# Moving 26 gate projections of a hybrid decoder layer out of its attention heads, into a stage of their own

## The chip, the cores and the metric

The kernel runs on one core of one Trainium2 chip. A core has five engines with an instruction stream each: TensorE (PE in the profile, its weight loads as PEld), VectorE (DVE), ScalarE (ACT), GpSimd (POOL) and SyncE (SP), which here issues nearly all DMAs. Each stream is carried out in order; engines meet at semaphores. The metric is the device time of one execution in microseconds (us), lower is better; the time of a kernel is the median of its runs.

## The reference

One layer of a decoder trunk, fp32, batch 1, 1024 tokens of 1024 channels with 16 meta tokens ahead of them (1040 in all). Cut to what matters:

```python
h = rms_norm(x_with_meta, norm_mix)
proj = h @ w_in + b_in
(g_q, g_k, g_v, g_r, g_lr, m_q, m_k, m_v, m_o, m_i, m_f, gate_a, gate_b) = jnp.split(proj, splits, axis=-1)
o_gla = head_rms(gla(g_q, g_k, g_v, log_a(g_lr))) * silu(g_r)          # 4 heads, keys 128, values 256
o_ml  = head_rms(mlstm(conv(m_q), conv(m_k), m_v, m_i, m_f)) * sigmoid(m_o)   # 4 heads
y = sigmoid(gate_a) * (o_gla @ w_branch_gla) + sigmoid(gate_b) * (o_ml @ w_branch_ml)
x = x + y @ w_out
x = x + conv_ffn(rms_norm(x, norm_ffn))     # 1024 -> 2 x 2816 -> 1024, causal conv of width 3
out = rms_norm(x, norm_final)[:, 16:]
```

`g_r`, `m_o`, `gate_a` and `gate_b` are the gates: 1024 channels each, so 32 tiles of 128 channels. None of them enters the recurrences; they multiply what comes out of them.

## The kernel before

**Numbers.** fp32 values are split into a high part H (rounded by a copy on ACT) and a low part L (the difference, on DVE); a product is three matmuls, H x H, H x L and L x H. A weight unit (8 x 128 rows, 128 columns, 512 KB) is loaded into `wr` (2 buffers, issued by SP), split into `wH` and `wL` (3 buffers each) by `prep` (lines 102 to 107), and used by `proj_cm` (line 158, PSUM tag `pj`, 3 banks): three thirds of the tokens, each 8 x 3 = 24 matmuls. `proj_v` (lines 188 to 205, `pv`, the same banks) computes values with the tokens as rows.

**Stages.** After norm and transposes (to about 36 us) come the heads (to about 890), GLA heads 0 to 3 and then mLSTM heads 4 to 7. For a head, `head_proj` projects k, q and v, `gate_proj` the two tiles of its output gate (`r`, `g_r` or `m_o`), `merge_gate("a", s)` a tile of gate a; behind the last head eight tiles of gate b. Small projections for decay and mLSTM's gates (`lr`, evicted into `raw_s` at line 445) follow head 0's keys and queries. Then the branch products `bg` (gate a times o_gla W) and `bm` (L986), w_out (`po`), the FFN's up stage (22 pairs of channel tiles, each as two pieces of seven block products V, X, Y, Z, a Winograd form of the 2x2 block product, L1186) and its down stage (from 1690).

**The recurrences** run beside the projections. `gla(s)` and `mlstm(s)` are generators in the list `side`; `main(gen)` lets one step of `side` follow each step of a projection. A GLA head computes the decay logits (`pre`, L643), ACT and DVE make the log decays `la` and their cumulative sum `bc` (L646 to L652), and then, for levels 1, 2, 4 ... 64, factors `pk` (L679, L680, L684 on DVE, L681 on ACT, L683 on POOL), scores `sc` (L620 on PE), and a masked merge into `A` (L637 on DVE). `sct` (L613) transposes A when the levels below 64 are merged; `kh`, `k`, `qh` (L706 to L722) are decayed keys and queries. `post` (its transposes have the tag `s`) multiplies the result by its norm and, on DVE, by the gate `r`, and stores it to `osc`; gate a and b go to `gsc`. `load_o` brings `osc` back for `bg` and `bm`.

**Order.** A list scheduler takes the program as written, with priorities (`hp(PRI_...)` moves an instruction ahead by so many places), and writes out each engine's order before the run; at run time nothing is reordered.

**down_sums** forms block differences of `ffn_w_down` for the last stage, on the side: 11 loads of 1 MB into `ts` (L927), four subtractions each (L929), and two stores (L931) to `tdn`, eight during the gate b tiles, three during `bg`.

## Time and profile before

| | |
|---|---|
| median of 3 runs | 1927.97 us (1926.66 to 1928.35) |
| span of the profiled execution | 1924.5 us |
| time of the profiled execution, by the median | about 3.5 us more than its span |
| instructions | 31317 |
| busy: PE, DVE, ACT, POOL | 1895.0, 1114.7, 807.0, 213.2 us |
| DMA | 244.69 MB, mean 127 GB/s |

How to read it: a profile is one execution. "Busy" is the time in which an engine had an instruction running. The chain that ended last is followed back from the last instruction to what released each step; its shares by engine say what the time was made of. A row of a timeline has the start, the time, engine, line, operation, output<-inputs, shapes and a count, and in square brackets the idle time before it and what ended it.

### The profile page before, as it was taken

The page shows a single profiled execution, that of the slowest core. Times are in us where ns is not written, and L with a number is a line of the kernel's source. Part 1 is how long each engine was busy: PE and PEld are TensorE (multiplying, and loading weights), DVE is VectorE, ACT ScalarE, POOL GpSimd, SP SyncE. Part 2 cuts the span into 40 slices and gives each one's busy share as a digit, 9 for nine tenths or more (in the row PEclk, how much of TensorE's full clock was granted, in tenths as well). Part 3 has the DMA queues.
Part 4 walks back from the last instruction along what each step waited for, and adds up shares of the span by engine and source line. Part 5 has one row for each costly group of instructions (what it writes and reads, how often), then busy time and mean ns, then how long its engine had stood idle before and what let it go on. Part 6 is the DMA issues. An engine that isn't in the chain of part 4 may idle for free.

```text
span 1924.5 us, 31317 instructions
## 1 busy us (share of the span) xinstructions
PE 1895.0 (98%) x13065; PEld 1815.8 (94%) x13065; DVE 1114.7 (58%) x1662; ACT 807.0 (42%) x1254; POOL 213.2 (11%) x189
## 2 busy tenths in 40 slices
PE   8999999999999999999999999999999999999998
PEld 8999999999999999999999999999999999987776
DVE  6272634437535433642251445688878788786777
ACT  5153444344534423323520234544444344455573
POOL 3030301103000000000000000012222222200000
PEclk8999999999999999999999999999999999999999
DMA  5121112021132122574971433323333333388794
GB/s 166 35 57 37 55 38 76 23 80 34 55 103 69 55 78 55 191 230 138 293 272 48 132 121 127 125 77 111 113 120 110 110 110 114 96 296 322 280 371 161
DMA packets 210568, 244.69 MB, mean 127 GB/s; under 512 B 11710, under 2 KB 170960, under 8 KB 210427
## 3 DMA queue, kind: packets, MB, share of 16 engines
q1 hardware_dynamic: 208587, 240.85, 38.9%
q8 instruction: 102, 1.67, 0.4%
q10 hardware_dynamic: 1840, 1.85, 0.3%
q14 instruction: 39, 0.32, 0.1%
HBM read 185.72 MB, written 56.95 MB: 126 GB/s over the span
## 4 chain that ended last, share of the span: by engine, by line
PE 78%; DVE 7%; issue 5%; DMA 5%; ACT 2%; POOL 2%; SPq 0%; POOLq 0%; DVEq 0%; ACTq 0%
PE pj L158 20%; PE pv L201 7%; PE Y L1186 6%; PE X L1186 6%; PE Z L1186 6%; PE bm L986 5%; PE bg L986 5%; PE po L1287 4%; PE V L1186 3%; PE pdX L1436 3%; PE pdY L1436 2%; PE pdZ L1436 2%; DMA ts<-in_ffn_w_down_dram 1%; PE pdV L1436 1%; DMA tdn<-ts 1%
## 5 line engine op out<-in xcount | busy, mean ns | idle before, releaser
L158 PE MATMUL pj<-xH,wH_r 128*128 128x342 f32 (+2 forms) x392 | 126.5, 323 | 0.0
L158 PE MATMUL pj<-xH,wL_r 128*128 128x342 f32 (+2 forms) x392 | 124.3, 317 | 0.0
L158 PE MATMUL pj<-xL,wH_r 128*128 128x342 f32 (+2 forms) x392 | 124.0, 316 | 0.0
L205 DVE TENSOR_TENSOR v<-pv,bB 128x256 f32<-128x256 f32 x64 | 27.1, 423 | 117.5 <-PE pv L201 117.5
L683 POOL TENSOR_TENSOR pk<-pk,kT 128x256 f32<-128x256 f32 (+1 forms) x40 | 58.9, 1500 | 183.0 <-ACT pk L681 104.8
L201 PE MATMUL pv<-wH_gv,xH 128*128 128x256 f32 x256 | 76.0, 297 | 0.0
L201 PE MATMUL pv<-wH_mv,xH 128*128 128x256 f32 x256 | 75.1, 293 | 0.0
L158 PEld LDWEIGHTS pj<-xH,wH_r 128*128 128x128 f32 x392 | 73.8, 188 | 0.1
L158 PEld LDWEIGHTS pj<-xL,wH_r 128*128 128x128 f32 x392 | 73.8, 188 | 0.1
L158 PEld LDWEIGHTS pj<-xH,wL_r 128*128 128x128 f32 x392 | 73.7, 188 | 0.0
L1287 PE MATMUL po<-wH_wo,yH 128*128 128x256 f32 x256 | 72.2, 282 | 0.1
L201 PE MATMUL pv<-wL_mv,xH 128*128 128x256 f32 x256 | 72.0, 281 | 0.0
L201 PE MATMUL pv<-wL_gv,xH 128*128 128x256 f32 x256 | 72.0, 281 | 0.0
L201 PE MATMUL pv<-wH_mv,xL 128*128 128x256 f32 x256 | 71.9, 281 | 0.0
L1287 PE MATMUL po<-wL_wo,yH 128*128 128x256 f32 x256 | 71.6, 280 | 0.3 <-DVE wL_wo L107 0.3
L201 PE MATMUL pv<-wH_gv,xL 128*128 128x256 f32 x256 | 71.9, 281 | 0.0
L1287 PE MATMUL po<-wH_wo,yL 128*128 128x256 f32 x256 | 71.8, 281 | 0.0
L1235 DVE SCALAR_TENSOR_TENSOR cv<-u,fc,cv 128x1024 f32<-128x1024 f32 x44 | 65.3, 1484 | 0.4
L158 PE MATMUL pj<-xH,wH_ga 128*128 128x342 f32 x192 | 62.5, 326 | 0.0
L158 PE MATMUL pj<-xH,wH_gb 128*128 128x342 f32 x192 | 61.9, 322 | 0.0
L986 PE MATMUL bm<-omH,wL_bm 128*128 128x342 f32 x192 | 61.5, 320 | 0.0
L158 PE MATMUL pj<-xH,wL_gb 128*128 128x342 f32 x192 | 61.4, 320 | 0.0
(674 smaller groups left out, 6755.1 us busy)
## 6 DMA issues: line engine op xcount, KB each, us to landing
ts<-in_ffn_w_down_dram SPq DMA_DIRECT2D x11, 1024.0 KB, 6.2
tdn<-ts SPq DMA_DIRECT2D x22, 512.0 KB, 2.7
rg<-in_ffn_w_up_dram SPq DMA_DIRECT2D x22, 512.0 KB, 3.8
ru<-in_ffn_w_up_dram SPq DMA_DIRECT2D x22, 512.0 KB, 3.9
adr<-s SPq DMA_DIRECT2D x40, 256.0 KB, 3.0
rd<-in_ffn_w_down_dram SPq DMA_DIRECT2D x20, 512.0 KB, 8.5
do<-tdn SPq DMA_DIRECT2D x18, 512.0 KB, 5.8
wr_r<-in_w_in_dram SPq DMA_DIRECT2D x16, 512.0 KB, 4.0
```

Source lines behind the costliest of these rows:

```text
L158: nc.tensor.matmul(pt[:, :n], a[:, k, :], b[:, k, base + t0:base + t0 + n], start=(i == 0), stop=(i == 3 * NK - 1))
L201: nc.tensor.matmul(pt[:, :DV], a[:, k, t0:t0 + P], b[:, k % 4, :], start=(i == 0), stop=(i == 3 * NK - 1))
L205: nc.vector.tensor_tensor(vt[:n, c, :DV], pt[:n, :DV], bB[:n, :], OP.add)
L683: nc.gpsimd.tensor_tensor(e, e, k, OP.mult)
L986: nc.tensor.matmul(pt[:, i, :n], a[:, k, :], b[k][:, t0:t0 + n], start=(k == 0 and j == 0), stop=(k == NK - 1 and j == 2))
L1186: nc.tensor.matmul(out[:, :n], a[:, k, :], b, start=start and k == 0 and j == 0, stop=stop and k == 3 and j == 2, skip_group_check=True)
L1235: nc.vector.scalar_tensor_tensor(y, u[:, j:SEQ + j], fc[:, j, jj:jj + 1], y, OP.mult, OP.add)
L1287: nc.tensor.matmul(pt[:, :DV], a, b[:, k % 4, :], start=(k == 0 and i == 0), stop=(k == NK - 1 and i == len(terms) - 1))
L1436: nc.tensor.matmul(banks[r, j, b], p, q, start=first and k == 0, stop=last and k == 2, skip_group_check=True)
```

## The change

Of the 32 gate tiles, 26 (all of `g_r`, `m_o` and gate a, and gate b's tiles 4 and 5) leave the heads. They become 13 pairs in a new stage between the heads and `bg`, in the block form of the FFN's up stage: `piece` and `product` are now shared by both, and a pair is 2 x 7 products of 12 matmuls with 258 or 256 columns. Gate b's other six tiles stay in the old form: `TAIL` (0, 1, 2) behind the last head, `COVER` (3) at the entry of the new stage, `END` (6, 7) at its exit.

- The block form needs differences of token blocks: `token_sums(k)` makes them on POOL (two adds of 1026 columns, four subtractions of 514) and stores them to `tsc` (4 DMAs per k, on SP); `token_blocks` loads and splits them at the stage's entry. It needs sums of weights too: `gate_weights`.
- Heads store their outputs without gates to `osc`; `post` evicts on ACT with a scale instead of on DVE with a multiply by `r`. `gate_finish` loads `osc` back, applies Silu or Sigmoid with the bias, multiplies, and stores to `otd`, which `load_o` reads. Gate a and b get their bias with the later Sigmoid.
- Head 1's keys are projected beside head 0's keys and queries, where the first gate tile was.
- `PACE = 1.7`: 1.7 steps of `side` for one step of a projection, where it was one.
- `down_sums` becomes `half_sums`: two per pair in the first 11 pairs of the new stage, 512 KB each, through one buffer `ts`.

```diff
-    uk, uq, uv, ur, uga, ugb = {}, {}, {}, {}, {}, {}
...
+    TAIL, COVER, END = (0, 1, 2), (3,), (6, 7)
     def head_units(s):
-        h = s % 4
-        kq_units(s)
+        h, g, k, q = s % 4, "gm"[s // 4], (O_GK, O_MK)[s // 4], (O_GQ, O_MQ)[s // 4]
+        if s != 1:
+            uk[s] = u_cm(w_in, k + P * h, f"{g}k{h}")
+        uq[s] = u_cm(w_in, q + P * h, f"{g}q{h}")
         if s == 0:
-            ur[0] = [u_cm(w_in, O_GR, "r0_0")]
+            uk[1] = u_cm(w_in, O_GK + P, "gk1")
             uk["lr"] = U.add()
-        uv[s] = u_v((O_GV if s < 4 else O_MV) + DV * h, f"{'gm'[s // 4]}v{h}_")
-    def gate_units(s):
-        h = s % 4
-        o = (O_GR if s < 4 else O_MO) + DV * h
-        ur.setdefault(s, []).extend(u_cm(w_in, o + P * j, f"r{s}_{j}") for j in range(len(ur.get(s, ())), 2))
-    head_units(0)
+        uv[s] = u_v((O_GV if s < 4 else O_MV) + DV * h, f"{g}v{h}_")
     for s in range(8):
-        if GATE_LATER[s]:
-            kq_units(s + 1)
-        gate_units(s)
-        if s < 7:
-            head_units(s + 1)
-        uga[s] = u_cm(w_in, O_GA + P * s, f"ga{s}")
-    for j in range(NK):
+        head_units(s)
+    for j in TAIL + COVER:
         ugb[j] = u_cm(w_in, O_GB + P * j, f"gb{j}")
...
+    def key_proj(s):
+        hh = heads.setdefault(s, {})
+        kT = hh["k"] = hd.tile([P, T + 3], F32, name=f"kT{s}", tag="k", bufs=2)
+        return proj_cm(uk[s], TH_ALL if s > 1 else SEG_ALL, 0, lambda p, t0, n: nc.scalar.activation(
+            kT[:, t0:t0 + n], p, AF.Identity, bias=cc(C_GK + s)))
...
             if s == 0:
-                yield from together(pk, pq, gate_proj(0, (0,)))
+                yield from together(pk, pq, key_proj(1))
...
+    tsc = dram.tile([4, 4, P, 514], F32, name="tsc")
+    def token_sums(k):
+        a, b = (hd.tile([P, T], F32, name=f"x{i}{k}", tag="r", bufs=2) for i in "ab")
+        t = wp.tile([P, T], F32, name=f"tx{k}", tag="gst", bufs=1)
+        for y, i in ((a, k), (b, k + 4)):
+            nc.gpsimd.tensor_tensor(y[:, :NP], xH[:, i, T0:].bitcast(F32), xL[:, i, T0:].bitcast(F32), OP.add)
+        first, second = slice(0, 514), slice(512, NP)
+        t1, t2 = t[:, 0:514], t[:, 520:1034]
+        for dst, x, y in ((t1, a[:, second], a[:, first]), (t2, b[:, second], t1),
+                          (a[:, second], b[:, second], a[:, second]), (b[:, first], b[:, first], t2)):
+            nc.gpsimd.tensor_tensor(dst, x, y, OP.subtract)
+        for i, src in enumerate((t1, t2, a[:, second], b[:, first])):
+            nc.sync.dma_start(tsc[i, k], src)
...
-                nc.vector.scalar_tensor_tensor(of[:, a:b], tp.rearrange("p n w -> p (n w)"), ncols[j],
-                                               r[:, a:b], OP.mult, OP.mult)
+                nc.scalar.activation(of[:, a:b], tp.rearrange("p n w -> p (n w)"), AF.Copy, scale=ncols[j])
...
+    PACE = 1.7
+    due = [0.0]
+    def main(gen, pace=PACE):
         for _ in gen:
-            advance()
+            due[0] += pace
+            while due[0] >= 1:
+                due[0] -= 1
+                advance()
...
-    def down_sums(m, t):
-        nc.sync.dma_start(t.rearrange("p (k i) n -> p k (i n)", k=2), wsrc(w_dn, 2 * m, 2, 0, D))
-        for o, a, b in ((0, 1, 0), (1, 3, 1), (3, 3, 0), (2, 2, 3)):
-            nc.vector.tensor_tensor(t[:, o], t[:, a], t[:, b], OP.subtract)
-        for i in range(2):
-            nc.sync.dma_start(tdn[i][m], t[:, 2 * i:2 * i + 2])
     main(head_proj(0))
     for s in range(8):
         side.append((gla if s < 4 else mlstm)(s))
         if s == 3:
             side.append(small_rows())
-        nxt = head_proj(s + 1) if s < 7 else iter(())
-        if GATE_LATER[s]:
-            main(islice(nxt, 6))
-        main(gate_proj(s, (0, 1) if s else (1,)))
-        main(nxt)
-        main(merge_gate("a", s))
-    ts = hd.tile([P, NC + 1, DV + 1], F32, name="ts", tag="v", bufs=2).rearrange("p a b -> p (a b)")
-    for j in range(NK):
-        down_sums(j, ts[:, :2048].rearrange("p (i n) -> p i n", n=512))
-        main(merge_gate("b", j))
+        if s > 3:
+            token_sums(s - 4)
+        if s < 7:
+            main(head_proj(s + 1))
+    for j in TAIL:
+        main(merge_gate_b(j))
...
+    def product(out, a, b, n, start, stop):
+        for k in range(4):
+            for j, (x, y) in enumerate(((a[0], b[0]), (a[0], b[1]), (a[1], b[0]))):
+                nc.tensor.matmul(out[:, :n], x[:, k, :], y[:, k, :], start=start and k == 0 and j == 0,
+                                 stop=stop and k == 3 and j == 2, skip_group_check=True)
+    def piece(pool, name, p, us_, u2, A, B):
+        n = (W0, W1)[p]
+        V, X, Y, Z = (pool.tile([P, 512], F32, name=f"{b}{name}_{p}", tag=f"{b}{p}") for b in "VXYZ")
+        ug, uu = us_
+        u2 = u2[:, p, :n]
+        g1, g2 = (u[:, W0 * p:W0 * p + n] for u in (ug, uu))
+        e1, e2 = (u[:, 514 + 256 * p:770 + 256 * p] for u in (ug, uu))
+        h2 = slice(n - 256, n)
+        def prod(out, a, b, start, stop):
+            product(out, A[a], B(b, p), n, start, stop)
+        prod(V, "A12", "B21", True, True)
+        prod(X, "A11", "B11", True, True)
+        with hp(PRI_E):
+            nc.scalar.activation(g1, V[:, :n], AF.Copy)
+            nc.vector.tensor_tensor(g1, X[:, :n], g1, OP.add)
+        yield
+        prod(Y, "S1", "T1", True, True)
+        prod(Z, "S3", "T3", True, True)
+        yield
+        prod(X, "S2", "T2", False, True)
+        with hp(PRI_E):
+            nc.scalar.activation(u2, X[:, :n], AF.Copy)
+            nc.vector.tensor_tensor(e2, Y[:, h2], u2[:, h2], OP.add)
+            nc.vector.tensor_tensor(e2, Z[:, h2], e2, OP.add)
+        yield
+        prod(Y, "S4", "B22", False, True)
+        prod(Z, "A22", "T4", False, True)
+        with hp(PRI_E):
+            nc.vector.tensor_tensor(e1, Y[:, h2], u2[:, h2], OP.add)
+            nc.vector.tensor_tensor(g2, Z[:, :n], u2, OP.add)
+        yield
...
+    GATES = [(O_GR + P * j, C_GR + j, AF.Silu, "g", j) for j in range(NK)] + \
+            [(O_MO + P * j, C_MO + j, AF.Sigmoid, "m", j) for j in range(NK)] + \
+            [(O_GA + P * j, None, None, "a", j) for j in range(NK)] + \
+            [(O_GB + P * j, None, None, "b", j) for j in range(NK) if j not in TAIL + COVER + END]
+    NG = len(GATES) // 2
...
+    def gate_weights(q):
+        rg, ru = (wp.tile([P, NK, P], F32, name=f"gw{i}{q}", tag="wr", bufs=2) for i in range(2))
+        for r, g in ((rg, GATES[2 * q]), (ru, GATES[2 * q + 1])):
+            nc.sync.dma_start(r, wsrc(w_in, 0, NK, g[0], P))
+        sa, sb = (gs.tile([P, NK, P], F32, name=f"gs{x}{q}", tag=f"S{x}") for x in "AB")
+        def split(src, h, l):
+            nc.scalar.activation(h, src, AF.Copy)
+            nc.vector.tensor_tensor(l, src, h.bitcast(F32), OP.subtract)
+        def two(src, name):
+            h, l = (wp.tile([P, NK, P], F32R, name=f"g{p}{name}_{q}", tag="w" + p) for p in "HL")
+            split(src, h, l)
+            return [(h[:, 4 * i:4 * i + 4], l[:, 4 * i:4 * i + 4]) for i in range(2)]
+        a = WP[q] = {}
+        a["A11"], a["A12"] = two(rg, "A1")
+        yield
+        nc.vector.tensor_tensor(sa[:, 0:4], ru[:, 0:4], ru[:, 4:8], OP.add)
+        nc.vector.tensor_tensor(sa[:, 4:8], rg[:, 0:4], ru[:, 0:4], OP.subtract)
+        a["S1"], a["S3"] = two(sa, "SA")
+        yield
+        nc.vector.tensor_tensor(sb[:, 0:4], sa[:, 0:4], rg[:, 0:4], OP.subtract)
+        nc.vector.tensor_tensor(sb[:, 4:8], rg[:, 4:8], sb[:, 0:4], OP.subtract)
+        a["S2"], a["S4"] = two(sb, "SB")
+        yield
+        t = gs.tile([P, NK, P], F32R, name=f"gA22_{q}", tag="A22")
+        a["A22"] = t[:, 0:4], t[:, 4:8]
+        split(ru[:, 4:8], *a["A22"])
+        yield
...
+    def token_blocks():
+        for i in (0, 2, 1, 3):
+            h, l = TB[i] = [gs.tile([P, 4, 514], F32R, name=f"T{p}{i}", tag=f"T{p}{i}") for p in "HL"]
+            nc.sync.dma_start(l.bitcast(F32), tsc[i].rearrange("k p c -> p k c"))
+            nc.scalar.activation(h, l.bitcast(F32), AF.Copy)
+            nc.vector.tensor_tensor(l, l.bitcast(F32), h.bitcast(F32), OP.subtract)
...
+    def gate_finish(q):
+        for i, u in enumerate(gu.pop(q)):
+            _, c, f, g, j = GATES[2 * q + i]
+            if f is None:
+                nc.sync.dma_start(gsc[g][j], u[:, :NP])
+                continue
+            o = gs.tile([P, T], F32, name=f"go{q}_{i}", tag="o")
+            nc.sync.dma_start(o[:, :NP], osc[g][j])
+            nc.scalar.activation(u[:, :NP], u[:, :NP], f, bias=cc(c))
+            nc.vector.tensor_tensor(u[:, :NP], u[:, :NP], o[:, :NP], OP.mult)
+            nc.sync.dma_start(otd[g][j], u[:, :NP])
+    def half_sums(m, c):
+        t = gs.tile([P, 4, 256], F32, name=f"ts{m}{c}", tag="ts")
+        for k in range(2):
+            nc.sync.dma_start(t[:, 2 * k:2 * k + 2], w_dn[P * (2 * m + k):P * (2 * m + k + 1), :].rearrange(
+                "p (i n) -> p i n", i=2)[:, :, 256 * c:256 * c + 256])
+        for o, a, b in ((0, 1, 0), (1, 3, 1), (3, 3, 0), (2, 2, 3)):
+            nc.vector.tensor_tensor(t[:, o], t[:, a], t[:, b], OP.subtract)
+        for i in range(2):
+            nc.sync.dma_start(tdn[i][m][:, :, 256 * c:256 * c + 256], t[:, 2 * i:2 * i + 2])
+    def gate_bank(name):
+        return lambda t0: psG.tile([P, 512], F32, name=f"{name}_{t0}", tag=f"{'XYZ'[t0 // 342]}1")
+    token_blocks()
+    with hp(PRI_W):
+        for _ in range(3):
+            weights_step(0)
+    for j in COVER:
+        main(merge_gate_b(j, gate_bank(f"pc{j}")))
+    weights_step(0)
+    u2 = wp.tile([P, T], F32, name="gu2", tag="gst", bufs=1)[:, :2 * W0].rearrange("p (a b) -> p a b", b=W0)
+    behind_ = None
+    for q in range(NG):
+        gu[q] = [gs.tile([P, T], F32, name=f"gu{i}{q}", tag=f"u{i}", bufs=2) for i in range(2)]
+        for p in range(2):
+            g = piece(psG, f"g{q}", p, gu[q], u2, WP[q], gate_block)
+            next(g)
+            if p == 1:
+                weights_step(q + 1)
+            next(g)
+            if p == 1:
+                weights_step(q + 1)
+            if behind_:
+                next(behind_)
+            if p == 0 and q:
+                weights_step(q)
+                weights_step(q)
+                gate_finish(q - 1)
+            next(g)
+            behind_ = g
+        if q < NP2:
+            for i in range(2):
+                half_sums(q, i)
+    next(behind_)
+    for j in END:
+        ugb[j] = u_cm(w_in, O_GB + P * j, f"gb{j}")
+    gate_finish(NG - 1)
+    for j in END:
+        main(merge_gate_b(j, gate_bank(f"pe{j}")))
+    gs_ctx.close()
...
-            nc.sync.dma_start(l.bitcast(F32), osc[g][k])
+            nc.sync.dma_start(l.bitcast(F32), otd[g][k])
```

144 lines of the change are left out of this document (47 added, 97 removed).

## The prediction

> **What bounds the kernel now.** I read the page first, then the chain of waits, then windows of single stages, then the timelines of the engines at the places that the change touches.
>
> ```profile
> span 1924.5 us, 31317 instructions
> PE 1895.0 (98%) x13065; PEld 1815.8 (94%) x13065; DVE 1114.7 (58%) x1662; ACT 807.0 (42%) x1254; POOL 213.2 (11%) x189
> PE 78%; DVE 7%; issue 5%; DMA 5%; ACT 2%; POOL 2%; SPq 0%; POOLq 0%; DVEq 0%; ACTq 0%
> ```
>
> TensorE (PE) is busy 98% of the span and holds 78% of the chain that ended last, so the kernel is as long as its matmuls, and the only room is to do fewer of them. It also means that a matmul taken out of a place where it covered a slower chain turns into idle time. The profiled execution has a span of 1924.5 us; the median of the runs is 1927.97, so 3.5 us lie outside the span, and I add them at the end. About 0.2% (4 us) is what a measurement can tell from no change.
>
> The windows show how tight the stages are. Columns are the length, then busy time and count of PE, PEld, DVE, ACT and POOL, then the granted PE clock, the DMA share and GB/s.
>
> ```profile
> 350.00:400.00 50.00, 50.00 (x359) 47.02 (x358) 18.52 (x38) 19.77 (x45) 2.93 (x6) 1.00 0.16 42
> 445.00:455.00 10.00, 10.00 (x72) 10.00 (x71) 10.00 (x12) 3.91 (x6) 6.34 (x5) 1.00 0.00 1
> 455.00:465.00 10.00, 7.64 (x52) 6.96 (x50) 8.43 (x10) 5.79 (x7) 0.10 (x1) 1.00 0.22 54
> 950.00:1000.00 50.00, 50.00 (x320) 50.00 (x319) 23.08 (x25) 18.17 (x21) 0.00 (x0) 1.00 0.90 300
> 1260.00:1270.00 10.00, 7.79 (x48) 7.58 (x48) 8.16 (x12) 2.50 (x3) 0.00 (x0) 0.78 0.09 26
> 1300.00:1350.00 50.00, 50.00 (x422) 50.00 (x422) 42.04 (x55) 24.44 (x31) 12.49 (x7) 1.00 0.35 106
> 1350.00:1400.00 50.00, 50.00 (x420) 50.00 (x420) 40.76 (x58) 17.65 (x24) 12.51 (x8) 1.00 0.40 125
> ```
>
> In the heads (350) PE is full while VectorE (DVE) has slack on average. But 445–465, in the last GLA head, shows the exception: DVE busy 10.00 of 10, and right behind it PE falls to 7.64.
>
> ```profile
> PE sct L613 <- DVE A L637: 2.4, 1, 2.4
> ```
>
> The waits of PE name it: the score transpose `sct` waited 2.4 us for the masked merge of A on DVE. The DVE chain of a GLA head already fills nearly all the time that its gate tiles give it. The change takes those tiles away.
>
> **A. Matmuls saved.**
>
> ```profile
> 868.81 11.31 PE pj L158 x72
> ```
>
> One gate tile is 72 matmuls of 342 columns, 11.31 us. 26 of them leave the old form: 294.1 us. A pair of tiles in block form is 2 pieces x 7 products x 12 = 168 matmuls of 258 or 256 columns, just as in the FFN's up stage, whose two windows above hold 422 + 420 = 842 matmuls in 100 us: 5.01 pairs, 19.96 us each. Thirteen pairs: 259.5. Saved: **34.6 us**, while everything that feeds them stays hidden. The six plain tiles of gate b cost what they did.
>
> **B. Startup: token sums ahead of a weight load, +17 (8 to 22).** In the changed kernel's instruction order all 24 `token_sums` instructions stand on GpSimd (POOL) right behind the mask building, and on SP's queue the 12 stores of k = 0 to 2 stand ahead of the load of `gq1`'s weights. In-order SP waits with them for POOL.
>
> ```profile
> 37.45 1.25 POOL L412 TENSOR_SCALAR_AFFINE_SELECT mfs<-mfs 128x64 f32<-128x64 f32 x2
> 1317.57 1.62 POOL L1164 TENSOR_TENSOR SB<-SA,rg 128x512 f32<-128x512 f32 x1 [12.68 <-issue]
> 1319.27 1.30 POOL L1165 TENSOR_TENSOR SB<-rg,SB 128x512 f32<-128x512 f32 x1
> 54.16 0.38 SPq L102 DMA_DIRECT2D wr_gk<-in_w_in_dram  x1
> 58.32 1.06 ACT L106 ACTIVATE wH_gk<-wr_gk 128x1024 fp32r<-128x1024 f32 x1 [2.24 <-DMA wr_gk<-in_w_in_dram]
> 65.28 0.55 ACT L445 ACTIVATE raw_s<-pj,bsm 96x346 f32<-96x346 f32 x1 [3.27 <-PE pj L158]
> wr_r<-in_w_in_dram SPq DMA_DIRECT2D x16, 512.0 KB, 4.0
> adr<-a SPq DMA_DIRECT2D x31, 256.0 KB, 2.2
> ```
>
> POOL is free at 38.7. An add of 512 columns takes (1.62 + 1.30) / 2 = 1.46, so a k with two adds of 1026 and four of 514 columns takes 2 x 2.9 + 4 x 1.5 = 11.8. Its buffers come free only as the stores of the k before land (2.2, of which some 0.9 hide behind the last add): +1.3. The third k ends at 38.7 + 3 x 11.8 + 2 x 1.3 = 76.7. Before, the load at that place was issued at 54.16. Now it goes out at about 77.2 and lands 4.0 later, 81.2. ScalarE (ACT), also in order, has the split of that weight (1.06) ahead of the evictions of key 1's last tile and of `raw_s`; it stops there, the three `pj` banks fill, and PE stops where the third `raw_s` tile would begin, at 65.2. ACT is free again at about 82.3, and the first bank at 82.8. Stall: 17 to 18. If POOL needs 0.9 per 512 columns instead, the third k ends some 10 us earlier (+8); if its waits for the stores are full, +22.
>
> **C. GLA heads: the cover is gone, +28 (8 to 45).** Head 1 of before, from the decay matmuls `pre` to the last merge that `sct` needs:
>
> ```profile
> 205.96 1.96 PE pre L643 x6
> 250.58 0.89 PE sc L620 x8
> 255.21 2.85 PE pv L201 x24
> 208.41 1.28 ACT L647 ACT_TABLE_LOAD   x1
> 213.29 1.37 DVE L650 SCALAR_TENSOR_TENSOR la<-pre,la 128x348 f32<-128x348 f32 x3 [9.41 <-ACT la L648]
> 219.93 0.42 DVE L679 TENSOR_TENSOR pk<-bc 128x256 f32<-128x256 f32 x1
> 222.47 1.35 DVE L637 COPY_PREDICATED A<-mu,sc 128x512 f32<-128x512 uint8 x1
> 224.59 1.21 DVE L680 TENSOR_TENSOR pk<-bc 128x512 f32<-128x512 f32 x1
> 230.97 1.31 DVE L637 COPY_PREDICATED A<-mu,sc 128x512 f32<-128x512 uint8 x1
> 232.08 0.72 DVE L680 TENSOR_TENSOR pk<-bc 128x512 f32<-128x512 f32 x1
> 234.59 1.27 DVE L712 TENSOR_TENSOR k<-bc 128x15 f32<-128x15 f32 x1
> 236.99 1.71 DVE L706 TENSOR_TENSOR kh<-bc 128x1024 f32<-128x1024 f32 x1
> 238.62 1.21 DVE L107 TENSOR_TENSOR wL_gv<-wr_gv,wH_gv 128x1024 fp32r<-128x1024 f32 x1
> 241.14 1.24 DVE L709 TENSOR_TENSOR kh<-kh,kT 128x1040 f32<-128x1040 f32 x1 [1.14 <-ACT kh L708]
> 242.91 1.21 DVE L722 TENSOR_TENSOR qh<-qh,qT 128x1024 f32<-128x1024 f32 x1
> 244.04 0.73 DVE L637 COPY_PREDICATED A<-mu,sc 128x512 f32<-128x512 uint8 x1
> 220.11 6.29 POOL L683 TENSOR_TENSOR pk<-pk,kT 128x256 f32<-128x256 f32 x4 [38.47 <-issue]
> ```
>
> DVE starts at 213.29, 7.3 after `pre` began, and is through at 244.77 with 31.5 us of nearly gapless work. What of it need not lie ahead of `sct`: one weight split (1.1 net), the `kh`, `k` and `qh` work with its gap (236.99 to 238.6, 239.8 to 242.3, 242.91 to 244.0, and the small op at 234.59; together 6.5) and 1.2 of the last level: 8.9. The changed order keeps one more split, 1.1, and one table load (1.28) falls away with the gates' Silu. `sct` can start 7.3 - 1.3 + 31.5 - 8.9 + 1.1 = 29.8 us after `pre`.
>
> PE's work between `pre` and `sct` in the changed order, at 0.157 us per 342-column matmul (11.31 / 72), 0.119 per 256-column one (2.85 / 24), 1.96 for `pre` and 5 x 0.89 for `sc`: head 0 has 48 and 79 (23.3), head 1 has 72 and 40 (22.5), head 2 has 96 and 18 (23.6), head 3 has 120 and none (25.3). The gaps are 6.5 + 7.3 + 6.2 + 4.5 = 24.5. Merges also wait for POOL and ACT in between; I followed head 2 by hand and came to 10.6 instead of 6.2, so the range reaches to 45, and I take 28, near the counted gaps. The low end comes from POOL. While POOL multiplied (220.11 to 226.4 and its followers), eight DVE instructions from 222.47 to 230.97 took some 0.5 longer than their like (1.21 against 0.72 for the same L680): 4 us. If the changed order lets them miss each other, the gaps are 2.5 + 3.3 + 2.2 + 0.5 = 8.
>
> The Trainium skill, "SBUF — State Buffer", section "Summary: rules for kernel authors", says that a DVE instruction with two SBUF inputs and a GpSimd one that reads SBUF exclude each other, the second waiting until the first finishes. By that rule it would wait for a whole multiply of 1.57 (6.29 / 4), more than the 0.5 that the row shows, and the chain would be some 8 us longer wherever they meet; the measured row is what I use.
>
> **D. mLSTM heads, +5 (0 to 15).** The end of a head (`op`, rms, transposes in `post`) is followed at once by the next head's with less projection between. Silu and Sigmoid leave ACT, but the four evictions per head move from DVE to ACT. No row shows this; between nothing and the 15 that four waits like C's smaller ones (4 x 3.5) make, I take the lower third.
>
> **E. The gate stage's side work, +16 (4 to 44).** Eleven of the 13 pairs carry two `half_sums` on one `ts` buffer: load 512 KB, four DVE subtractions, store 512 KB, and only then the next load. SP does this in order, with weight loads, `o` loads and output stores between.
>
> ```profile
> rg<-in_ffn_w_up_dram SPq DMA_DIRECT2D x22, 512.0 KB, 3.8
> tdn<-ts SPq DMA_DIRECT2D x22, 512.0 KB, 2.7
> ogL<-oscg SPq DMA_DIRECT2D x8, 513.0 KB, 7.1
> ```
>
> A half is 3.8 + 1.7 (four subtractions of 256 columns at 0.42, the row at 219.93) + 2.7 + issues = 8.5. The second one also waits for the `o` load, about 3.2 more: 20.2 in all against PE's 19.96. The changed DVE order puts the second half's first subtraction ahead of the low-part split of SB, which PE needs for the next pair, so lateness reaches PE. Traffic is ten transfers' worth of 512 KB, 5.1 MB per 20 us, 256 GB/s, where the row at 950 shows 300 GB/s at a share of 0.90 and the FFN row at 1350, from which 3.8 comes, only 0.40; transfers will be slower than 3.8. I take 1.5 us in each of 11 pairs. At 7.1 per transfer in one place of four it is 4 a pair, 44.
>
> **F. Entry and exit, +2 (0 to 8).** Sigmoid with bias costs the same. The stage's entry needs stored heads and token blocks back; one plain tile (11.31) covers. Two tiles (22.6) cover the outputs' reload (7.1 each, overlapped).
>
> **Sum.** -34.6 + 17 + 28 + 5 + 16 + 2 = +33.4; 1924.5 + 33.4 + 3.5 = **1961 us**.
>
> **Rivals.** *The chains fit* (faster). POOL and DVE miss each other, so `sct` is ready within 26 us of `pre`, POOL's adds are quick, and the `ts` loop ends inside 19.96: -34.6 + 13 + 8 + 0 + 4 + 0 = -10, 1918; with B at 8, 1913. I call it 1916. It decides where all stalls together stay under 34.6. For it: PE at 98% in before with every one of these chains; against: the 2.4 us wait at 455 with the gates still there. *The store loop sets the stage's pace*: E at 44 instead of 16 gives 1989. For it: 256 GB/s wanted; against: the 300 GB/s at 950 with PE full. *The clock falls behind each stall*: the window at 1260 has a clock of 0.78 behind PE's gaps, a loss of 2.2 in 10 us; five long stalls (B and C) make +11, 1972. Against: the 2.4 us wait at 455 left the clock at 1.00.
>
> The Trainium skill, "TensorE: Matmul & The Clock Gate", section "Part 1: The HAM clock gate (the "warmup" mystery)", has the clock at half after an idle window of about 3.4 us until a busy one; by that, five stalls cost an estimated 1.7 each, 8.5. [...]
>
> **How the numbers follow.** Forecast 0.50 (its own range 1935 to 1990), chains fit 0.18, no change 0.03 (between the two), store loop 0.17, clock 0.12. All ends worst at once would be far out; the upper deviations taken as independent (5, 17, 10, 28, 6) make 35, 1997, and the clock a little more: high 2000. Low 1912, the fitting case nearly to its end. Faster 0.19, same 0.03, slower 0.78.
>
> **What would show it.** Right: a stop of PE of 15 us or more near 65, while POOL runs `token_sums` and `wr_gq1` is issued only behind their stores; four waits of `sct` for the merge of A, 4 to 11 each; gate pairs of 20 to 22 us, with waits of the SB products for DVE's split. Wrong: no stop near 65; `sct` waits below 3 us; gate pairs of 20.0, or of 23 and more; a granted clock below 1.00 for long behind the stops.

## The result and the profile after

The changed kernel takes 2013.93 us (median of 4 runs, 2011.35 to 2019.91) against 1928.16: a ratio of 1.0451, 95% interval 1.0433 to 1.0469. It is 86 us slower where 33 were forecast, and it lies above the top of the range (2000). The side was right, the size was not.

The top of the page after, and the core's granted clock (before it was 0.994):

```profile
span 2009.6 us, 32599 instructions
PE 1895.8 (94%) x13377; PEld 1807.0 (90%) x13377; DVE 1227.3 (61%) x1902; ACT 827.7 (41%) x1280; POOL 242.2 (12%) x213
```

```profile
core 0: 2009.6 us, clock 0.976
```

Two things are to be seen. PE's idle time went from 1924.5 - 1895.0 = 29.5 us to 2009.6 - 1895.8 = 113.8: 84.3 more. And PE's busy time is the same as before, although 34.6 us of matmuls were saved: the matmuls that are left took some 35 us longer than their count accounts for (26 of them are found below, in the clock; 9 stay unassigned). 84.3 + 35.4 - 34.6 = 85.1, the difference of the spans.

What PE waited for, the largest groups (us in total, times, longest):

```profile
PE Xg L933 <- DVE gLSB L993: 25.4, 8, 6.9
PE pj L158 <- ACT kT L414: 16.4, 1, 16.4
PE ot L554 <- DVE or L545: 12.6, 5, 6.0
PE sc L601 <- POOL pk L664: 12.3, 8, 3.1
PE sc L601 <- DVE pk L665: 9.3, 8, 2.1
```

None of these was above 1.0 us in all before. In order: the gate stage's low part of SB (E of the prediction), the startup (B), the transposes of the heads' outputs (in D and C), and the GLA heads' scores (C, two rows).

By stages: from 40 us to the first decay matmul, GLA heads, mLSTM heads with four plain tiles, the gate stage from its first product to `bg`, and the rest (columns as in the prediction).

```profile
40.00:117.00 77.00, 60.63 (x460) 60.16 (x458) 14.05 (x16) 10.09 (x16) 41.92 (x26) 0.89 0.27 80
117.00:418.20 301.20, 275.14 (x1822) 251.43 (x1822) 173.26 (x284) 139.37 (x253) 56.93 (x56) 0.98 0.13 38
418.20:708.40 290.20, 279.12 (x1872) 264.59 (x1871) 132.44 (x308) 119.77 (x225) 11.77 (x12) 0.98 0.24 69
708.40:1041.60 333.20, 299.54 (x2329) 295.87 (x2328) 203.10 (x351) 108.09 (x143) 0.41 (x1) 0.95 0.71 211
1041.60:1970.00 928.40, 917.48 (x6544) 879.26 (x6545) 645.71 (x836) 408.69 (x565) 111.73 (x73) 1.00 0.47 159
```

Before, the first decay matmul began at 97.4, and `bg` at 957.8 (rows of those tiles). Startup: 117.0 - 97.4 = **+19.6**. Heads: before, 860.4 us lay between the two, with 31 gate tiles (350.6) and head 1's keys (11.4, now ahead of it); the changed heads, with four plain tiles of 11.31, should take 543.6 up to the gate stage's first product and take 708.4 - 117.0 = 591.4: **+47.8**. Gate stage: 13 pairs of 19.96 and two plain tiles are 282.1; it takes 333.2: **+51.1**. After `bg`: **+1.3**. Together 119.8; less the saved 34.6 that is 85.2.

**The clock.** A short wait in the gate stage, in windows of 1 us; the third number from the end is the granted clock:

```profile
814.00:815.00 1.00, 0.47 (x5) 0.28 (x3) 0.32 (x1) 0.67 (x2) 0.00 (x0) 1.00 0.40 131
815.00:816.00 1.00, 0.00 (x0) 0.00 (x0) 1.00 (x2) 0.00 (x0) 0.00 (x0) 1.00 0.01 4
816.00:817.00 1.00, 0.70 (x5) 0.70 (x6) 1.00 (x4) 0.39 (x1) 0.00 (x0) 1.00 0.00 0
817.00:818.00 1.00, 1.00 (x10) 1.00 (x9) 1.00 (x3) 0.90 (x2) 0.00 (x0) 0.89 0.00 0
818.00:819.00 1.00, 1.00 (x7) 1.00 (x7) 1.00 (x2) 0.28 (x2) 0.00 (x0) 0.50 0.82 247
820.00:821.00 1.00, 1.00 (x7) 1.00 (x6) 0.00 (x0) 0.00 (x0) 0.00 (x0) 0.50 1.01 291
821.00:822.00 1.00, 1.00 (x10) 1.00 (x9) 0.43 (x1) 0.62 (x1) 0.00 (x0) 0.90 1.11 423
```

PE is idle for 1.8 us in all and then works again, and the clock falls to 0.50 behind the wait, for 3.4 us: 7 matmuls in a microsecond where 11 ran before the wait. Read in windows of 0.5 us from 40 to 1042, the changed kernel has 87.2 us of idle PE and loses 26.2 us to the clock (PE's busy time by one minus the clock); the kernel before has 4.1 and 0.0. By place these are 2.5 at the start, 11.0 in the heads and 12.8 in the gate stage. There are 13 such drops, at a cost of 1.5 to 3.1 each, behind 13 of the 22 idle stretches of 1.5 us and more; none stands behind a shorter one alone.

Which waits are followed by a drop is mostly not a matter of chance. All changes of the granted clock in this trace lie on one grid of 3.41 us. In the steps of this grid, the wait above (814.37 to 821.20), and then the prediction's wait of 2.4 us in the kernel before (458.87 to 469.11):

```profile
814.37:817.79 3.42, 1.60 (x13) 1.49 (x13) 3.10 (x7) 1.46 (x2) 0.00 (x0) 1.00 0.03 9
817.79:821.20 3.41, 3.41 (x18) 3.41 (x18) 2.20 (x5) 0.77 (x2) 0.00 (x0) 0.50 0.84 234
```

```profile
458.87:462.29 3.42, 2.22 (x19) 2.02 (x17) 3.38 (x4) 2.75 (x3) 0.00 (x0) 1.00 0.14 40
462.29:465.70 3.41, 2.25 (x13) 1.77 (x14) 2.31 (x3) 1.06 (x2) 0.10 (x1) 1.00 0.02 5
465.70:469.11 3.41, 3.41 (x32) 3.41 (x31) 1.95 (x4) 2.37 (x5) 0.00 (x0) 1.00 0.00 0
```

The first wait lies in one step, which has 1.82 us of idle PE, and the next step has half the clock. The second, though longer, is cut in two by the grid, 1.20 and 1.16, and no drop follows. Over the 16 traces of this case, from 40 us on, 189 drops each follow a step with about 1.5 us or more of idle PE (1.49 is the least); of the 159 steps at full clock with 1.9 us or more, 158 are followed by one, and between 1.5 and 1.9 both are found. So a short wait costs clock or not by where the grid cuts it.

### The profile page after: what moved, and what is told of

It reads as the page before. It is cut to its first block, busy times and chain, and to the rows that moved or that the text cites. A ratio compares the mean times of both kernels' runs of the same rounds, so it can differ in the third digit from the quotient of the medians.

```text
span 2009.6 us, 32599 instructions
## 1 busy us (share of the span) xinstructions
PE 1895.8 (94%) x13377; PEld 1807.0 (90%) x13377; DVE 1227.3 (61%) x1902; ACT 827.7 (41%) x1280; POOL 242.2 (12%) x213
## 5 line engine op out<-in xcount | busy, mean ns | idle before, releaser
L664 POOL TENSOR_TENSOR pk<-pk,kT 128x256 f32<-128x256 f32 (+1 forms) x40 | 47.6, 1210 | 158.3 <-ACT pk L662 96.1
L1136 PE MATMUL bg<-ogH,wH_bg 128*128 128x342 f32 x192 | 61.5, 320 | 1.5 <-ACT gb L450 1.5
L1057 DVE TENSOR_TENSOR ts<-ts 128x256 f32<-128x256 f32 x88 | 37.1, 421 | 40.5 <-DMA ts<-in_ffn_w_down_dram 38.4
L1136 PE MATMUL bm<-omH,wH_bm 128*128 128x342 f32 x192 | 61.4, 320 | 0.0
L1136 PE MATMUL bg<-ogL,wH_bg 128*128 128x342 f32 x192 | 61.4, 320 | 0.0
L1136 PE MATMUL bg<-ogH,wL_bg 128*128 128x342 f32 x192 | 61.3, 319 | 0.0
L1136 PE MATMUL bm<-omL,wH_bm 128*128 128x342 f32 x192 | 61.3, 319 | 0.0
L1309 POOL TENSOR_TENSOR SB<-SA,rg 128x512 f32<-128x512 f32 x20 | 32.1, 1607 | 235.9 <-issue 114.1
L933 PE MATMUL Xg<-TH,gLSB 128*128 128x258 f32 (+1 forms) x104 | 32.7, 315 | 25.6 <-DVE gLSB L993 25.4
L601 PE MATMUL sc<-pk 128*128 128x128 f32 x224 | 32.6, 291 | 24.2 <-POOL pk L664 12.3
```

What stands on the lines that cost most here:

```text
L601: nc.tensor.matmul(pt[:, i, :], pk[:, P * i:P * (i + 1)], pk[:, 512 + P * i:512 + P * (i + 1)], start=True, stop=True)
L664: nc.gpsimd.tensor_tensor(e, e, k, OP.mult)
L933: nc.tensor.matmul(out[:, :n], x[:, k, :], y[:, k, :], start=start and k == 0 and j == 0, stop=stop and k == 3 and j == 2, skip_group_chec ...
L1057: nc.vector.tensor_tensor(t[:, o], t[:, a], t[:, b], OP.subtract)
L1136: nc.tensor.matmul(pt[:, i, :n], a[:, k, :], b[k][:, t0:t0 + n], start=(k == 0 and j == 0), stop=(k == NK - 1 and j == 2))
L1309: late.tensor_tensor(sb[:, 0:4], sa[:, 0:4], rg[:, 0:4], OP.subtract)
```

## The experiments

Each run is one profiled execution beside timed runs. The table gives for each the median, the start of the first decay matmul, and how much the heads (first decay matmul to the gate stage's first product) and the gate stage (from there to `bg`) took over their matmuls, counted as above with 19.96 per pair and 11.31 per plain tile.

| run | median us | first decay matmul | heads over | gate stage over |
|---|---|---|---|---|
| changed kernel | 2013.9 | 117.0 | 47.8 | 51.1 |
| e1 sums late | 2028.9 | 96.9 | 79.9 | 53.9 |
| e4 one plain tile per GLA head | 2004.9 | 98.4 | 66.8 | 41.8 |
| e5 two ts buffers | 2003.8 | 116.3 | 48.4 | 41.9 |
| e6 two o buffers | 2011.8 | 116.7 | 47.8 | 51.6 |
| e7 sums stored by POOL | 2000.7 | 98.7 | 47.4 | 56.8 |
| e8 two plain tiles, 1.14 steps | 1998.2 | 99.0 | 35.8 | 60.0 |
| e9 half sums in heads | 1994.3 | 98.2 | 88.1 | 16.1 |
| e10 e7 + e8 + e9 | 1981.5 | 98.6 | 73.2 | 7.4 |
| e11 half sums: subtractions on POOL | 2042.2 | 117.4 | 48.4 | 81.3 |
| e12 half sums all on POOL | 1998.4 | 117.7 | 51.7 | 36.7 |
| e13 e7 + e8 + e12 | 2012.5 | 98.9 | 36.1 | 72.0 |
| e14 e13, later transposes | 2035.6 | 99.0 | 57.9 | 75.8 |
| e15 one half sum per pair, e7 | 1972.0 | 97.8 | 49.4 | 31.0 |
| e16 e15 with tiles in GLA heads | 1975.6 | 99.2 | 53.4 | 27.5 |

Without the room that e5 and e6 free, a second buffer does not fit: the gate stage would need 104.6 KB per partition, and 103.5 are left (e2 and e3, which gave no time).

In e4, e8, e9, e10, e13, e14 and e16 the order also moved token sums from the start into the heads, because their buffers were taken by then; that by itself frees the start and burdens the heads, as e1 shows, so their heads' column holds two effects.

**Startup.** First the token sums were held back:

```diff
-            token_sums(s - 4)
+            with tc.issue_after(heads[s]["one"].ins):   # POOL's memset of v in head s
+                token_sums(s - 4)
```

> Same work; the 24 GpSimd instructions of the token sums (and so their stores on SP's queue) come behind GLA head 2 and later instead of at the start. Theory: SP's queue held the load of gq1's weights behind the stores, the 16.4 us wait of PE for ACT's key eviction and the clock of 0.51 and 0.63 in the two windows of 10 us around it (another 4 us) go: about 1993. Rival: PE only waits a little later for the first decay matmuls instead, no more than 5 us are gained: 2009.

The startup's wait went, and `pre` began at 96.9. But the kernel became 15 us slower. POOL in this run, and PE's waits for the transposes of the heads' outputs:

```profile
410.33 2.40 POOL L461 TENSOR_TENSOR xa<-xH,xL 128x1026 f32<-128x1026 f32 x1
422.17 3.17 POOL L466 TENSOR_TENSOR xb<-xb,tx 128x514 f32<-128x514 f32 x1
425.30 1.81 POOL L93 TENSOR_TENSOR rs3r<-rs3v,mhalf 128x9 f32<-128x9 f32 x1
```

```profile
PE ot L554 <- DVE or L545: 39.0, 9, 11.2
```

The small power for head 3's norm (L93) stands behind 15 us of token sums, and the norm, its products on DVE and the transposes wait with it: 39.0 us instead of 12.6. So the place at the start was not the fault; what it did to SP was. The next run keeps the place and takes the stores from SP:

```diff
-            nc.sync.dma_start(tsc[i, k], src)
+            nc.gpsimd.dma_start(tsc[i, k], src)
```

> Same work and the same place for the token sums on GpSimd, at the start; only their 16 stores are issued by GpSimd itself instead of SP. Theory: SP is free for gq1's weights, the 16.4 us wait at the start goes together with the low clock behind it, and unlike in the run with late sums nothing stands ahead of the reciprocal roots that GpSimd makes at the end of each head (waits of the transposes for them stay at 13 to 17): about 1992. Rival (the wait was for GpSimd, not for the queue): a wait of 10 us or more stays at the start, 2008.

As the theory had it: `pre` at 98.7, the transposes' waits still 12.6, clock 1.00 up to there. The start gained 18.3, of which 16.4 were the wait; the gate stage behind it took 5.7 more, and the kernel gained 13.3.

**GLA heads.** One plain tile of gate b in each:

```diff
+        if s < len(GLA):                       # GLA = (0, 1, 4, 5)
+            main(merge_gate_b(GLA[s]))
         if s < 7:
             main(head_proj(s + 1))
```

> Gate b's tiles 0, 1, 4, 5 in the old form, one in each GLA head between its projections and the next head's; 12 pairs in block form instead of 13, one tile (2) left behind the last head. Costs 2.7 us of matmuls. Theory: the GLA heads' chain on DVE and POOL gets 11.3 us more of PE's work to hide behind, PE's waits at the score matmuls (24 us with their POOL and DVE releasers, and some 6 of clock) fall below 8: 2009.6 + 2.7 - 22 + 3.5 = about 1993. Rival (the chain is as late in any case, since its steps follow PE's own: the plain tile stands before it and not beside it): waits stay, 2015.

The theory as I put it failed: the score matmuls waited 30.7 us, not under 8. (The total fell since the token sums left the start in this order, and the startup wait with them.) In heads 0 to 2, away from the token sums, they waited 6.3, 6.9 and 5.9, in the changed kernel 4.7, 5.9 and 6.3. The order shows why: between `pre` and `sct` stood 21.5 us of matmuls at streaming speed, as in the changed kernel (19 to 22). The scheduler sets `sct` where the side generator's steps put it, 1.7 per projection step; a tile more doesn't change that. The next run changes the steps as well:

```diff
-            main(head_proj(s + 1))
+            main(head_proj(s + 1), 1.14 if s < 4 else PACE)    # and two gb tiles ahead of it, paced alike
```

> All eight tiles of gate b in the old form, two in each GLA head ahead of the next head's projections, and 1.14 steps of the recurrence for one of the projections there instead of 1.7; gate a's tiles 0, 1, 6, 7 take gate b's old places around the new stage; 10 pairs in block form. Costs 8 us of matmuls against 13 pairs (6 tiles at 11.31 for 3 pairs at 19.96). In the order PE then has 33 us of work between the decay matmuls and the score transpose, where the changed kernel has 19 to 22 and the run with one plain tile and 1.7 steps had 21.5. Theory (chain of some 30 us against PE's supply of work up to it; it is the steps per projection, not the tiles alone, that set the supply): the waits of the score matmuls fall from 24 (31 with one plain tile) below 8, and about 25 us with the clock are gained, and some 20 more if the startup's wait is gone too, as it was with one plain tile: 2013.9 + 8 - 25 - 20 = about 1977. Rival (the score waits come from GpSimd's multiplies being slow for what the order allows them, step by step): waits stay above 18, about 1998.

```profile
PE bg L1141 <- ACT ogH L1124: 19.1, 1, 19.1
...
PE sc L604 <- DVE pk L668: 5.7, 4, 2.1
...
PE sc L604 <- POOL pk L667: 3.8, 5, 0.8
```

With 33 us of matmuls between `pre` and `sct` the scores waited 9.5 us, 24 before the edit, and the heads' loss fell by 12. It was paid back at the stage's exit: the 10 pairs had to take the eleven pairs' half sums, the last two behind the last pair, and the reload of the head outputs stood behind them (19.1). So C's chain-against-supply mechanism holds, and the steps per projection are its knob, at 8 us of matmuls for 12 gained.

**Gate stage.** The row that the prediction asked for, in one pair: SP's half sum issues, DVE, and PE.

```profile
873.74 1.25 SPq L1054 DMA_DIRECT2D ts<-in_ffn_w_down_dram  x2
878.83 1.48 SPq L1059 DMA_DIRECT2D tdn<-ts  x2
884.92 1.25 SPq L1054 DMA_DIRECT2D ts<-in_ffn_w_down_dram  x2
899.08 1.50 SPq L1054 DMA_DIRECT2D ts<-in_ffn_w_down_dram  x2
887.95 0.43 DVE L1057 TENSOR_TENSOR ts<-ts 128x256 f32<-128x256 f32 x1 [7.09 <-DMA ts<-in_ffn_w_down_dram]
888.29 1.22 DVE L993 TENSOR_TENSOR gLSB<-gsB,gHSB 128x1024 fp32r<-128x1024 f32 x1
889.57 0.58 PE L933 MATMUL Xg<-TH,gLSB 128*128 128x258 f32 x1 [6.78 <-DVE gLSB L993]
```

The load at 884.92 waits for the stores of 878.83 to land; DVE stands 7.09 us at the subtraction that needs it; the low part of SB comes right behind, and PE has waited 6.78. From 873.74 to 899.08 a pair's two half sums take 25.3 us (24.0 is the mean over the nine pairs from 750 to 966), where PE's pair is 19.96. The runs change the parts of this chain. A second `ts` buffer, and a second `o` buffer in the same room:

```diff
-        sa, sb = (gs.tile([P, NK, P], F32, name=f"gs{x}{q}", tag=f"S{x}") for x in "AB")
+        sa, sb = gs.tile([P, NK, P], F32, name=f"gsA{q}", tag="SA"), rg
...
-        t = gs.tile([P, 4, 256], F32, name=f"ts{m}{c}", tag="ts")
+        t = gs.tile([P, 4, 256], F32, name=f"ts{m}{c}", tag="ts", bufs=2)      # e5; for e6 the o tile instead
```

> Same work as the changed kernel; SB is written over the spent weight tile rg, and the 4 KB that this frees give the buffer ts of the half sums a second one. Theory: the next ts load waits on SP for the stores of the one before, DVE stops at the half sum's first subtraction, and the low part of SB is late behind it: PE's 25.4 us of waits for it fall below 8, and with the lower clock behind them 25 to 35 us are gained: about 1984. Rival (the stage's 210 GB/s are all that the transfers get, whatever the buffers): waits stay above 18, gain under 8: 2006.

> Same work; SB over rg as in the run with two ts buffers, but the freed room goes to a second buffer for the stored head outputs (o). Theory (ts is the one that holds SP): gain under 8 us, 2006. Rival (SP is held by the o loads, which wait for the buffer until its product is formed): waits for the low part of SB fall below 12, gain of 15 and more: 1997.

```profile
PE Yg L933 <- ACT gHSA L992: 7.7, 3, 3.0
...
PE Yg L933 <- DVE gLSA L993: 6.5, 6, 1.4
...
PE Xg L933 <- DVE gLSB L993: 3.4, 2, 3.2
```

With two `ts` buffers (the rows) SB's low part waits 3.4 instead of 25.4, as the theory said, but SA's parts, whose weights now land after 7.0 us (5.3 before the edit), wait 14.2: 10 us gained, not 25 to 35. With two `o` buffers the waits for SB's low part fell to 5.2, which was the rival's sign, but others came in their place and the time stayed (2 us less, the theory's number). Neither expectation holds whole: waits move within the stage. Both runs also write SB over `rg`, and SB's waits fell in both, so how much of that fall the second `ts` buffer made, and whether SA's lateness came with the shared edit, is not shown. Then the subtractions alone went to POOL, and then the loads and stores too:

```diff
-            nc.vector.tensor_tensor(t[:, o], t[:, a], t[:, b], OP.subtract)
+            nc.gpsimd.tensor_tensor(t[:, o], t[:, a], t[:, b], OP.subtract)     # e11; e12: also nc.gpsimd.dma_start
```

> The changed kernel, with only the four subtractions of each half sum (88 in all) moved from VectorE to GpSimd, which is idle in the gate stage; loads, stores, the single ts buffer and SP's order stay. Theory (VectorE, in order, stands at a subtraction whose ts load is late, with the low part of SB behind it): the waits for the low part of SB fall from 25 to under 6, as with two ts buffers, but waits for weights behind SP's ts load stay or grow (the run with two ts buffers had 14 us of waits for SA): stage 315 to 322 instead of 333, total about 1998. Rival (SP's queue alone is to blame): the same low part is late by its weights, stage 328 and more.

> The same, with the half sums' loads and stores issued by GpSimd's queue too, so that neither VectorE nor SP ever waits for a half sum. Theory: both ways in which the half sums reach PE are gone, and the traffic is as before: the stage comes to 296 to 305, as without half sums in it (298), total about 1980. Rival (the traffic itself delays the weights, 210 GB/s and more): 315 and more, total 1996.

e11 cleared SB's waits and made the stage 30 us longer: POOL's subtractions are slower (4.7 to 5.0 us for four at 864.91 and 890.39; DVE's take 0.42 each), SP, still in order, stands at their stores until POOL is done (80.6 us in all), and the weights behind it came later (21.8 and 11.3 us of waits for SA's parts). The stage took 363.4, past the rival's 328. That SP's order carries at least as much of the harm as DVE's is an argument from it and not shown, since the loop itself became longer too. In e12 neither waits for a half sum, and the stage's loss is 36.7 instead of 51.1, not the 14 to 23 of the theory: with 318.8 the stage has the rival's sign (315 and more). DVE waited 15.6 us for weight loads there (3.2 in e9 below, which has no half sums in the stage), although these land after a median of 4.6 us in both; what makes them late stays open. POOL in e12, a load at the start of each half sum:

```profile
850.55 1.44 POOL L1054 DMA_DIRECT2D ts<-in_ffn_w_down_dram  x2 [6.14 <-DMA tdn<-ts]
863.16 1.44 POOL L1054 DMA_DIRECT2D ts<-in_ffn_w_down_dram  x2 [2.42 <-DMA tdn<-ts]
880.18 1.44 POOL L1054 DMA_DIRECT2D ts<-in_ffn_w_down_dram  x2 [4.71 <-DMA tdn<-ts]
894.61 1.44 POOL L1054 DMA_DIRECT2D ts<-in_ffn_w_down_dram  x2 [5.03 <-DMA tdn<-ts]
```

14.7 us for each, so that 22 of them fill the whole stage. What they cost by being there at all is told by taking them out, into heads 5 to 7 (each held back by a copy of four columns from a tile just projected):

```diff
-                half_sums(q, i)                                   # gate stage
+            if halves and count[0] % 2 == 0:                       # every other projection step of heads 5 to 7
+                half_sums(*halves.pop(0))
```

> Same work as the changed kernel; the 22 half sums are made during the projections of heads 5 to 7 (two buffers there, each held back by a copy of 4 columns from a tile just projected) instead of in the gate stage. Theory: the gate stage's loss over its 293 us of matmuls (333.2 measured, so 40) is the traffic and the order on SP that the half sums bring: it falls to under 303, less 30 to 35, of which the mLSTM heads give back 5 to 10, since VectorE and SP get the work there: about 1987. Rival (the stage's other loads and stores, or its weight sums, are late by themselves): the stage stays above 318, total 2005 or more.

```profile
729.90:1028.10 298.20, 290.85 (x2330) 287.17 (x2329) 170.93 (x258) 105.97 (x142) 0.41 (x1) 0.99 0.55 159
```

The gate stage then has 7.3 us of idle PE and a clock of 0.99, and its loss is 16.1. The heads pay 40 for it, four times what I gave them and more: DVE, in order, now stands at the subtractions there, with the mLSTM chain behind it: matmuls of that chain (`op`, `msc`) wait 15.7 us for DVE, and nothing in the changed kernel. Three of the four token sums are among the heads too, but the transposes that they held up in e1 wait only 16.1 us here (12.6 in the changed kernel).

```profile
DVE ts L924 <- DMA ts<-in_ffn_w_down_dram: 46.5, 24, 6.9
```

One half sum per pair, the rest beside the last plain tiles and the first `bg` products:

```diff
-            for i in range(2):
-                half_sums(q, i)
+            half_sums(*halves.pop(0))       # 13 here, 3 at TAIL's tiles, 6 in bg
```

> The changed kernel with token sums stored by GpSimd, and the 22 half sums spread: 3 beside the last three plain tiles of the heads, 13 in the gate stage (one per pair, one buffer as before), 6 beside the first products with the GLA branch weights, where the kernel before had three of its eleven. Theory (the rate: two half sums take 25 us of a 20 us pair, one takes 11 to 14): the gate stage comes to within 10 us of its 282 of matmuls from the first product on, instead of 333 to 339, and 2000.7 - 45 = about 1958. Rival (any half sum in the stage delays the weights on SP's queue): stage above 310, total above 1975.

The loss is 31.0: with none, one and two half sums per pair it is 16.1, 31.0 and 51.1 (56.8 with e7's stores). So half sums cost something even where they do not outgrow the pair's 20 us: the 13 of one per pair cost 14.9, 1.1 each. The nine more of the changed kernel cost 20 to 26, so 2.2 to 2.9 each. Both expectations missed: the stage is above the rival's 310, the total, 1972, below its 1975. It is the fastest variant found, still 2.35% above the kernel before (ratio 1.0235, 1.0215 to 1.0256).

**Together.** In order e10, e13, e14 and e16. The run before e14 is e13, and the run before e16 is e15.

> Three measures at once: token sums stored from GpSimd's queue, two plain gate b tiles in each GLA head with 1.14 side steps there, half sums in heads 5 to 7. 10 pairs in block form (+8 us of matmuls against 13 pairs). Theory, additive: startup -18, GLA heads -25 + 8, gate stage -30 (10 pairs, so 8 less of it: -23), mLSTM heads +7: 2014 - 51 = about 1963. Were the stalls the whole loss it would have to come below 1928 only with those of the mLSTM heads gone as well. Rival (stalls move on: a wait taken away is found again at the next place): above 1985.

> Three measures that touched different stages: token sums stored by GpSimd, two plain gate b tiles per GLA head with 1.14 side steps, half sums on GpSimd with its own queue; 10 pairs in block form. By stages as measured or expected: 98.6 to the first decay matmul, 358 in the GLA stage, 289 in the mLSTM heads, 235 in the gate stage with its three plain tiles, 957 after: 1938 span, 1941. Rival (stalls move on): above 1960.

> As the run before, with three more steps of the side generator between the norm's multiplications on VectorE and the transposes of each head's output on PE, which wait there 12 to 17 us in five heads. Theory (the order has the transposes too early for the real chain ACT, GpSimd, VectorE): these waits fall below 5, 10 us and some clock are gained: 1929. Rival: the heads' side work ends later for the added steps and the next head's chain waits instead: 1941 and more.

> As the run before, with one plain gate b tile in each GLA head and 1.37 side steps there (24 to 29 us of PE's work between decay matmuls and score transpose, where the changed kernel has 19 to 22), 12 pairs in block form, one plain tile behind the last head; half sums 1, 13 and 8. Theory: GLA's score waits fall from 24 to about 12 and some of the low clock with them, -15 for 2.7 of matmuls: about 1945, still slower than the kernel before by 1%, for the waits that stay in the heads. Rival (waits only move): no better than the run before.

e10 came to 1981, inside neither theory nor rival: the gate stage is clean (7.4), and the heads took all of the half sums' cost. In e13 POOL's half sums were not done when the 10 pairs were:

```profile
PE bg L1141 <- ACT ga L453: 50.7, 1, 50.7
```

and POOL's timeline there:

```profile
1024.63 1.44 POOL L1059 DMA_DIRECT2D ts<-in_ffn_w_down_dram  x2 [2.39 <-DMA tdn<-ts]
...
1034.66 0.40 POOL L1167 MEMSET yM<- 128x366 f32 x1 [1.92 <-DMA tdn<-ts]
```

The last of them ended at 1034, and `bg` began at 1040.7, most likely since its tiles take the place of the stage's buffers (that was argued, not tried apart). e14's later transposes (three more `yield`s in `post`) cut their waits from 14.6 to 7.5 and brought 32 us of waits of the scores for POOL, on which token sums stand from 414 to 457 in that run. The rival, a later chain, had that right. e16 (2.5% above before, median of four runs) shows GLA's score waits at 12.7, as expected, and nothing gained: `sct` itself now waits 11.9, and the heads are over by 53.4 instead of 49.4, with the token sums among them. The rival, that waits only move, had it right.

## Why the prediction went wrong

**A, the matmuls: right.** The gate stage without half sums, e10's 10 pairs, came within 7.4 us of 222 at 19.96 a pair. What was saved is real.

**B, the startup: right to 1 us.** The stores and the load that waited behind them, SP in the changed kernel, and ACT's split:

```profile
75.24 0.32 SPq L468 DMA_DIRECT2D tsc<-xb  x1
75.66 0.39 SPq L102 DMA_DIRECT2D wr_gq<-in_w_in_dram  x1
80.96 1.06 ACT L106 ACTIVATE wH_gq<-wr_gq 128x1024 fp32r<-128x1024 f32 x1 [24.05 <-DMA wr_gq<-in_w_in_dram]
```

76.7, 77.2 and 81.2 were forecast; the stall is 16.4 (17 forecast), and with the clock behind it the start is 19.6 late. The size is in part luck: the first three k took POOL 10.0, 12.0 and 9.8, not 11.8 each, and its waits for stores were 2.6 and 1.7, not 1.3. The low end of the range was summed wrongly: at 0.9 per 512 columns three k are 13.8 shorter and not 10, so it was +3, not +8; C's lower gaps add up to 8.5, not 8. Neither bears on the forecast.

**C and D, the heads: 33 forecast, 47.8 measured.** The idle time in the heads' two windows is 26.1 + 11.1 = 37.2, near the forecast; the other 10.6 is the clock (11.0 by the count above). C's length of the chain was right: `sct` began 30.9 to 31.8 after `pre` (29.8 forecast), and the waits add up to 24.2 over the four heads (24.5 counted, 28 taken), though they stood at `sc`, the matmuls that feed A, and not at `sct`. Of the 12.6 at the transposes, 11.1 lie in the mLSTM window (6.0 of them for head 3's output), where D was given 5.

**E and F, the gate stage: 18 forecast, 51.1 measured.** This is the term that was sized wrongest. I put a half sum pair at 20.2 us from transfer times of the FFN stage and of the kernel before's `down_sums`, and took 1.5 of lateness; it took 25.3 in the pair above. A pair of the stage took 23.9 on the average ((333.2 - 22.6) / 13), and 23 and more was named as a sign of being wrong. The issues of the stage in the changed kernel, median us to landing last:

```profile
ts<-in_ffn_w_down_dram SPq DMA_DIRECT2D x44, 256.0 KB, 3.2
tdn<-ts SPq DMA_DIRECT2D x44, 256.0 KB, 4.3
...
go<-oscg SPq DMA_DIRECT2D x8, 513.0 KB, 7.6
```

The store of 256 KB landed after 4.3 us, where I had taken 2.7 from a 512 KB store of the kernel before, and the `o` load after 7.6 (5.8 for the mLSTM heads' outputs), where I had given it 3.2 more. The rival "the store loop sets the stage's pace", at 44, priced it well and had 0.17; its against, 300 GB/s at 950 with PE full, looked at throughput, where the loop is one of latencies. The loop's pace is only part of it, as e15 shows, where half sums cost 15 us below that pace. That they cause most of the loss is shown by taking them out (16.1 in e9, 7.4 in e10); how it divides between SP's order, DVE's order and the transfers beside them is not.

**The clock: nothing in the sum, 26 us measured.** It was a rival of its own at 11, as if it excluded the others; but it follows from every case with waits, so it belonged into the sum as a price on each wait. It was sized by five long stalls; there were 13 drops, 9 of them behind waits shorter than 3.4 us. The row I set against it, a wait of 2.4 us that left the clock at 1.00, was a wait that the grid cut in two: of the six stretches of 2.0 to 2.5 us in both kernels up to `bg`, three have a drop. The row I had for it, at 1260, held the answer: its two drops follow waits of 2.0 and 2.2 us. The Trainium skill, "TensorE: Matmul & The Clock Gate", section "Part 1: The HAM clock gate (the "warmup" mystery)", has the clock at half after an idle window of about 3.4 us; its one half is what the rows show (0.50), but 9 of the 13 drops here followed idle stretches of less than 3.4 us, the shortest of them 1.6. The measurement decides.

Taken together: the mechanisms of B, C and E were found before the run, and the step that failed is the pricing of E, a loop of transfers priced by times from other stretches and then given 1.5 us of lateness a pair, with the clock left out of the sum. The gate stage (33 short of its 51, 13 of it clock) and the heads (15 short, 11 of it clock) make 48 of the 52 us that were missed.

## What to carry to other kernels

Where a kernel is bound by matmuls that also hide a serial chain, count the chain against the matmuls that stay next to it before taking any away: 34.6 us of saved matmuls uncovered 84 us of waits. Price side work in a stage by the latency of its loop (load, compute, store landing, next load) at that stage's traffic, and look at what stands behind it in order on every queue it uses. Add the clock to each wait of TensorE: here 9 of 18 waits between 1.5 and 3.5 us, and all four longer ones, were followed by another 1.5 to 3 us lost at half clock, as the grid cut them.

## What the hardware showed unexpectedly

The clock gate acts on waits much shorter than I had taken: drops to 0.50 behind 9 of the 18 idle stretches of 1.5 to 3.5 us in the changed kernel, for one or two steps of 3.41 us, beginning 1.8 to 3.5 us after the wait began, so that for most of these waits PE is at work again by then. What decided was not the length of the wait but the idle time in one step of the grid: 1.9 us and more was followed by a drop in 158 of 159 steps of all traces. In the kernel before, with one stretch above 1.5 us in these stages, which the grid cut in two, there were none. And a store of 256 KB landed after 4.3 us (`tdn<-ts`) in the gate stage at 211 GB/s, another one (`adr<-a`) after 2.2 in the FFN stage at half of that.
